# Half of the tokens first at the layer change, T's blocks by ScalarE's queue, and a new order of states, exponentials and the last gates

## The chip, the core and the metric

The kernel runs on one core of a Trainium2 chip. A core has five engines that each follow their own fixed list of instructions: TensorE (PE in the profile; PEld is its weight load), VectorE (DVE), ScalarE (ACT), GpSimd (POOL) and SyncE (SP), which only issues DMAs. ScalarE and GpSimd can issue DMAs as well. An instruction waits, by semaphores, until what it reads is there and what it overwrites has been read; what stands behind it on its engine waits with it. Matrix products go to PSUM (eight banks of 512 floats for each of 128 partitions), all else lies in SBUF or in HBM. The metric is the time of one execution on the device, in microseconds.

## The reference

512 tokens of 2048 floats pass two residual layers, x <- x + W_out(mixer(RMSNorm(x)) * silu(gate)), in float32. The first is differential attention with eight heads. The second is RWKV-7 time mixing with 32 heads of 64: one projection gives r, k, v, the gate g and two narrow streams of 96 columns (decay and learning rate), each mixed with the token before; then, for each head and token, a 64 x 64 state is updated.

```
p = h @ w_in;  p = p + (token_shift(p) - p) * mu
r, k, v, g, dw, da = split(p)
decay = exp(-exp(-softplus(-(w0 + tanh(dw) @ decay_up)) - 0.5))
a = sigmoid(a0 + da @ iclr_up)
kk = normalised(k * k_k);  k = k * (1 + (a - 1) * k_a)
S = S * decay + (S @ -kk) (kk * a)^T + v k^T;   y = S @ r      # token by token
y = group_norm(y) * gn_w + gn_b + sum(r * k * r_k) * v
x = x + (y * silu(g)) @ w_out
```

## The kernel before

**Products.** All large products take float32 data as a high and a low part in TensorE's reduced float32 format and make three products of them (`mm3`, L114): high x high, high x low, low x high. Weights come by SyncE's queue as 512 KB blocks (`wraw`), ScalarE casts the high part (`wh`, L102), VectorE subtracts it (`wl`, L103). The normalised activations stand as 16 blocks of 128 channels by 512 tokens (`hH`, `hL`), which both layers' projections read.

**Order.** A planner places each engine's instructions ahead of time by priorities: `high_priority(offset)` moves a piece forward by AHEAD (2000), SCAN (3000) or SOLVE (4000), and `issue_after` pins it behind an instruction. Work of the scan is strung in between the projections' products by a count: each `mm3` product is a tick, and a `Chain` makes its next step after a given number of ticks (L127 to L173).

**The start.** TensorE makes a few products of the identity (`warm`, L616) before the first block of x is there, two more after the first block's transposes.

**The layer change.** The last part of attention's W_out ends with `seven`, which forms half of the output columns by a scheme of seven block products; `store_x` stores each finished tile of the residual by ScalarE's queue (L725) and sums its squares on ScalarE (L727). VectorE makes the reciprocal root of the norm for tokens 0 to 255 and then for 256 to 511 (L774 to L777) and scales x by it (L770). `more_h` transposes a block of 128 channels, all four token tiles, on TensorE (L790); `make_h` writes hH on ScalarE (L811) and hL on VectorE (L812); `unit_chan` multiplies each block by the 192 columns of the two narrow streams (tile `lora`).

**A pair of heads.** Layer 1 goes over 16 pairs of heads. For pair j its k, r and v are projected, then `stage1` makes the decay's cumulative sums and exponentials; three pieces of it (`decays`, `queries`, `keys`) stand in a list `later`, and one piece is issued after each state of the scan that is running. `gram` multiplies keys and queries in chunks of 64 tokens (tile `gp`, L1021), copies the result to G on ScalarE (L1028), and sends six small pieces to HBM by GpSimd's queue (`ltd`, L1034 and L1040); GpSimd then masks G in four instructions (L1046, L1048). `t_solve` loads the pieces back in another layout by four DMAs of GpSimd (`LT`, L1071) and inverts triangular blocks of 32 in 31 steps of two VectorE instructions (`tmpl` L1082, `Tm` L1084); the result goes to HBM (`td`, L1086). In the next pair's turn `t_combine` loads it (`TT`, L1098, SyncE), transposes it on VectorE (L1106), multiplies on TensorE (`px`, L1112 and L1122), and copies back on ScalarE (L1115, L1118, L1125).

**The scan.** `scan_pair` walks over eight chunks. Each has a product (`sm`, L1193), its copy on ScalarE (`rhs`, L1196), a product with T (L1204), its copy (`VS`, L1206), a product (L1211) and the new state on VectorE, one instruction for each of two heads (L1215; L1218 in the first chunk), with a copy and a scaling on GpSimd (`SA` L1199, `Sg` L1202). `outputs` and `centre` follow, then `group_norm`, `finish_y` and the gate.

**The last projections.** After pair 15 the gates of pairs 13, 14 and 15 are projected and the rows of the gated output are split again into high and low parts (`split_row`, L421 and L422, into the buffers of hH and hL): rows 0 to 13 from HBM (`yr`), rows 14 and 15 from the gates directly. Then W_out is applied.

Of the kernel before, what the change touches and what calls it, by code (L numbers as in the profile page):

```python
# [23 lines left out]
P = 128  # L24
# [14 lines left out]
AHEAD, SCAN, SOLVE = 2000, 3000, 4000  # L39
# [552 lines left out]
def layer0(g, aps):  # L592
# [3 lines left out]
    with ExitStack() as cx:  # L596
# [46 lines left out]
        def more(n, m):  # L643
            for k in range(len(g.hH), min(n, KT)):
# [5 lines left out]
                if k == 0:  # L650
                    warm_up(2, last.ins)
# [27 lines left out]
    with ExitStack() as cx:  # L679
# [43 lines left out]
        def store_x(cb, t):  # L723
            xr = xs[cb][:, t, :]
            nc.scalar.dma_start(out=g.xd[t * P : (t + 1) * P, cb * 512 : cb * 512 + 512], in_=xr)  # L725
            junk = g.work.tile([P, 512], F32, name="junkx", tag="a", bufs=2)
            nc.scalar.activation(junk[:], xr, AF.Square, accum_out=g.ssx[:, t, cb : cb + 1])  # L727
# [77 lines left out]
def make_h(g, ps, col):  # L805

    nc = g.nc
    hh = g.hp.tile([P, T], F32R, name="hH", tag="hH")
    hl = g.hp.tile([P, T], F32R, name="hL", tag="hL")
    w = g.prm_a[:, col : col + 1]  # L810
    m = nc.scalar.activation(hh[:], ps[:], AF.Copy, scale=w)  # L811
    d = nc.vector.scalar_tensor_tensor(hl[:], ps[:], w, hh[:].bitcast(F32), ALU.mult, ALU.subtract)  # L812
    g.hH.append(hh)
    g.hL.append(hl)
    return m.ins, d.ins
# [128 lines left out]
def stage1(g, j, k, up):  # L944
# [24 lines left out]
    def decays():  # L969
# [3 lines left out]
        nc.vector.tensor_sub(l[:], l[:], m[:, :, None].to_broadcast([P, NC_, C]))  # L973
        nc.scalar.activation(p.E[:, :, 0], m[:], AF.Exp, scale=-1.0)
# [20 lines left out]
    g.later += [decays, queries, keys]  # L995
# [14 lines left out]
def gram(g, j, p, before):  # L1010
# [33 lines left out]
    for h in range(2):  # L1044
        r_ = slice(h * C, h * C + C)
# [16 lines left out]
def t_solve(g, j, p):  # L1062
# [7 lines left out]
    for i in range(NG):  # L1070
        nc.gpsimd.dma_start(out=LT[i * 32 : i * 32 + 32], in_=g.ltd[j % 2].rearrange("b h c s t -> (b h c) s t"))  # L1071
# [14 lines left out]
    nc.gpsimd.dma_start(out=g.td[j % 2].rearrange("q l t -> l q t"), in_=Tm[:])  # L1086

# [4 lines left out]
def t_combine(g, j, p):  # L1092
# [11 lines left out]
    for h in range(2):  # L1104
        r_ = slice(h * C, h * C + C)
        nc.vector.transpose(T1[r_], TT[r_, :, h, 0:HALF])  # L1106
# [47 lines left out]
def gate(g, j, gps):  # L1154
    nc, w = g.nc, g.work
    gt = shift_mix(g, gps, P, *mus(g, 3, j), "v", 1)
# [6 lines left out]
def gated(g, j, p, gt, last=False):  # L1163
    g.nc.vector.tensor_mul(gt[:], gt[:], p.y[:])
    if last:
        return split_row(g, gt[:])
# [15 lines left out]
def scan_pair(g, j, p, gap, gap_s, others):  # L1182
# [8 lines left out]
    for c in range(NC_):  # L1191
# [20 lines left out]
        for h, r_ in HEADS:  # L1212
            s_ = sm[r_, o + h * C : o + h * C + C]
            if c:
                g.state = nc.vector.scalar_tensor_tensor(VS[r_, c + 1, h, :], s_, p.gam[r_, c : c + 1], Sg[r_, :],  # L1215
                                                         ALU.mult, ALU.add)
            else:
                nc.vector.tensor_scalar(VS[r_, c + 1, h, :], s_, p.gam[r_, c : c + 1], None, ALU.mult)  # L1218
# [22 lines left out]
def centre(g, p):  # L1241
# [4 lines left out]
    for h in range(2):  # L1246
# [3 lines left out]
        nc.vector.tensor_sub(p.yc[:, h::2, :], yg, s1[:, :, h : h + 1].to_broadcast([P, NT, C]))  # L1250
# [25 lines left out]
def layer1(g, aps):  # L1276
    nc, tc = g.nc, g.tc
    with ExitStack() as cx:
# [23 lines left out]
        for j in range(D // P):  # L1302
# [13 lines left out]
            def behind(m, j=j, p=p):  # L1316
# [4 lines left out]
                t_solve(g, j, p)  # L1321
# [18 lines left out]
        gt = gate(g, j - 1, gps)  # L1340
        row = []

        def last_but_one(m):
            with tc.issue_after(m.ins):
                finish_y(g, j - 1, pairs[j - 1])
                row.append(gated(g, j - 1, pairs[j - 1], gt, True))

        gt = gate(g, j, proj(3, j, behind=(24, last_but_one)))
        rows = split_rows(g, g.yd2, ("r", "k", "th0", "th1", "l", "f", "xH", "xL"), 1, j - 1) + row

        def all_rows(n, _):
            if n >= KT and len(rows) < KT:
                group_norm(g, j, p)
                finish_y(g, j, p)
                rows.append(gated(g, j, p, gt, True))
# [56 lines left out]
def body(ctx, tc, nc, aps):  # L1412
    g = Ctx()
    g.nc, g.tc = nc, tc
    g.last, g.first = None, []
# [40 lines left out]
```

## Time and profile before

| what | before |
|---|---|
| median of three runs | 2207.12 us (2206.14 to 2209.69) |
| profiled execution | 2213.33 us, span 2211.6 us |
| mean granted TensorE clock | 0.990 |
| busy: TensorE, VectorE, ScalarE, GpSimd | 98%, 65%, 47%, 16% of the span |

The profile gives, for one execution, each engine's busy time, the waits by who ended them, and a timeline. A row of the timeline shows the start and length in us, engine, source line, operation, output and inputs, the shape, how many instructions are merged (x4), and in brackets the idle time of the engine before it and what ended that. Matmuls are pipelined, and their ends are modelled. The columns of the views that are quoted below are told where they stand.

### The profile page before, as it was taken

To read this page: it belongs to the slowest core of one execution; us is meant where nothing else is said; L and a number is where in the kernel's file an instruction comes from. 1 tells how busy PE (TensorE), PEld (TensorE's weight loads), DVE (VectorE), ACT (ScalarE), POOL (GpSimd) and SP (SyncE) were. 2 spreads that over 40 slices of the span, in tenths; PEclk is the share of its full clock that TensorE was granted. 3 is DMA by queue.
4 is the path that set the end of the run, shared out by engine and by line. 5 is a ranking of instruction groups with operands and counts; after the bars stand their busy time and mean duration, and the time that the engine had idled before them with its cause. 6 is when DMAs were issued, how large, how long until landed. Compare 5 with 4: busy or idle time off the path is not lost. (4 is left out here: it accounts for less than half of the span.)

```text
span 2211.6 us, 33922 instructions
## 1 busy us (share of the span) xinstructions
PE 2173.2 (98%) x12202; PEld 1762.5 (80%) x12202; DVE 1445.7 (65%) x3772; ACT 1040.9 (47%) x2110; POOL 359.8 (16%) x733
## 2 busy tenths in 40 slices
PE   9999999999999999989999999999999999999999
PEld 7888888888888878867777777778777777777887
DVE  5664646455564666465677788677777777777645
ACT  6443434344343454335455555555555556545322
POOL 0000000000000000110233233333332233331001
PEclk9999999999999999999999999999999999999999
DMA  6322232222222356643422333333333332345456
GB/s 192 97 85 97 77 102 89 87 95 86 96 86 95 129 183 213 162 106 90 106 67 78 79 92 86 82 91 94 98 91 82 89 88 75 107 131 182 174 166 120
DMA packets 281401, 240.21 MB, mean 109 GB/s; under 512 B 31792, under 2 KB 239744, under 8 KB 281232
## 3 DMA queue, kind: packets, MB, share of 16 engines
q1 hardware_dynamic: 256912, 190.13, 28.5%
q0 software_dynamic: 15456, 31.90, 6.7%
q10 hardware_dynamic: 8864, 16.01, 2.0%
q8 instruction: 96, 1.57, 0.3%
q14 instruction: 73, 0.60, 0.1%
HBM read 217.98 MB, written 19.99 MB: 108 GB/s over the span
## 5 line engine op out<-in xcount | busy, mean ns | idle before, releaser
L103 DVE TENSOR_TENSOR wl<-wraw,wh 128x1024 fp32r<-128x1024 f32 (+2 forms) x319 | 388.8, 1219 | 360.9 <-ACT wh L102 353.9
L102 ACT CAST wh<-wraw 128x1024 fp32r<-128x1024 f32 (+2 forms) x319 | 333.4, 1045 | 535.3 <-PE pp L114 374.5
L114 PE MATMUL pp<-wh,hH 128*128 128x512 f32 x1268 | 499.8, 394 | 4.0 <-ACT hH L421 2.4
L114 PE MATMUL pp<-wl,hH 128*128 128x512 f32 x1268 | 498.0, 393 | 0.0
L114 PE MATMUL pp<-wh,hL 128*128 128x512 f32 x1268 | 497.7, 393 | 0.0
L114 PE MATMUL pp<-hL,wh 128*128 128x512 f32 x1024 | 417.6, 408 | 0.0
L114 PE MATMUL pp<-hH,wl 128*128 128x512 f32 x1024 | 417.1, 407 | 0.0
L114 PE MATMUL pp<-hH,wh 128*128 128x512 f32 x1024 | 412.1, 402 | 0.0
L114 PEld LDWEIGHTS pp<-wh,hH 128*128 128x128 f32 x1268 | 238.6, 188 | 52.9 <-ACT hH L421 2.8
L114 PEld LDWEIGHTS pp<-wh,hL 128*128 128x128 f32 x1268 | 238.5, 188 | 47.9
L114 PEld LDWEIGHTS pp<-wl,hH 128*128 128x128 f32 x1268 | 238.8, 188 | 46.7
L114 PEld LDWEIGHTS pp<-hH,wh 128*128 128x128 f32 x1024 | 195.1, 191 | 37.0 <-issue 1.2
L114 PEld LDWEIGHTS pp<-hL,wh 128*128 128x128 f32 x1024 | 194.8, 190 | 35.2
L114 PEld LDWEIGHTS pp<-hH,wl 128*128 128x128 f32 x1024 | 195.0, 190 | 31.4
L1082 DVE SCALAR_TENSOR_TENSOR tmpl<-LT,Tm 128x60 f32<-128x60 f32 (+24 forms) x496 | 133.1, 268 | 10.6
L459 POOL DMA_DIRECT2D frow<-yd x12 | 8.9, 739 | 796.4 <-DVE rs_i L63 676.6
L1199 POOL COPY SA<-VS 64x64 f32<-64x64 f32 x224 | 61.2, 273 | 428.2 <-DVE VS L1215 382.9
L1084 DVE TENSOR_TENSOR Tm<-Tm,tmpl 128x60 f32<-128x60 f32 (+24 forms) x496 | 104.2, 210 | 11.2
L1215 DVE SCALAR_TENSOR_TENSOR VS<-sm,gam,Sg 64x64 f32<-64x64 f32 x192 | 54.2, 282 | 50.9 <-PE sm L1211 46.5
L1196 ACT COPY rhs<-sm 64x64 f32<-64x64 f32 x256 | 52.8, 206 | 63.6 <-PE sm L1193 61.1
L1206 ACT COPY VS<-sm 64x64 f32<-64x64 f32 x256 | 52.8, 206 | 62.0 <-PE sm L1204 58.3
L1202 POOL TENSOR_SCALAR Sg<-SA,gam 128x64 f32<-128x64 f32 x96 | 72.9, 759 | 9.3
(326 smaller groups left out, 3224.0 us busy)
## 6 DMA issues: line engine op xcount, KB each, us to landing
wraw<-in_rw_w_in_dram SPq DMA_DIRECT2D x128, 512.0 KB, 3.8
wraw<-in_da_w_in_dram SPq DMA_DIRECT2D x254, 256.0 KB, 2.9
wraw<-in_da_w_out_dram SPq DMA_DIRECT2D x26, 512.0 KB, 4.4
wraw<-in_rw_w_out_dram SPq DMA_DIRECT2D x26, 512.0 KB, 3.9
LT<-ltd POOLq DMA_DIRECT2D x64, 132.0 KB, 2.9
yr<-yd SPq DMA_DIRECT2D x28, 256.0 KB, 3.5
frow<-yd POOLq DMA_DIRECT2D x12, 512.0 KB, 6.9
xq<-in_x_dram SPq DMA_DIRECT2D x16, 256.0 KB, 5.7
```

The lines of the kernel that those rows point to most:

```text
L102: nc.scalar.copy(hi[:, ks], raw[:, ks])
L103: nc.vector.tensor_sub(lo[:, ks], raw[:, ks], hi[:, ks].bitcast(F32))
L114: m = nc.tensor.matmul(out, a, b, start=s, stop=e, skip_group_check=skip)
L459: nc.gpsimd.dma_start(out=r, in_=src[k0 * P : (k0 + KG) * P, :].rearrange("(k p) t -> p k t", p=P))
L1082: nc.vector.scalar_tensor_tensor(tt, LT[:, i : i + 1, i + 1 :].to_broadcast([P, s, n]), n2[:, i : i + 1], Tm[:, 0:s, i : i + 1].to_broadca ...
L1084: nc.vector.tensor_add(Tm[:, 0:s, i + 1 :], Tm[:, 0:s, i + 1 :], tt)
L1196: nc.scalar.copy(rhs[r_, :], sm[r_, h * C : h * C + C])
L1199: nc.gpsimd.tensor_copy(p.SA[r_, c - 1, :], VS[r_, c, h, :])
L1202: nc.gpsimd.tensor_scalar(Sg[:], p.SA[:, c - 1, :], p.gam[:, c : c + 1], None, ALU.mult)
L1206: nc.scalar.copy(VS[r_, c, h, :], sm[r_, P : P + C])
L1215: g.state = nc.vector.scalar_tensor_tensor(VS[r_, c + 1, h, :], s_, p.gam[r_, c : c + 1], Sg[r_, :], ALU.mult, ALU.add)
```

## The change

1. The warm-up behind the first transposes grows from two products to seven.
2. `store_x` sums the squares before it issues the store, and for the last 1024 columns with priority SCAN.
3. At the layer change the first eight blocks are made and multiplied for tokens 0 to 255, then for 256 to 511 (`half_h`, `products`); blocks 8 to 15 as before. A PSUM tile then holds two blocks of two token tiles.
4. The exponentials leave `decays` for a piece of their own (`exps`), so that `later` has four pieces.
5. The six stores of `gram` go by ScalarE's queue; the masks become `mask_gram`, called for one head before `t_solve` and for the other behind its loads.
6. T's transposes in `t_combine` are pinned behind the last `centre` of the scan before.
7. The new state is placed with priority STATE (8000), ahead of the rows of T (SOLVE, 4000).
8. The last gate has a buffer of its own (tag E), and the rows of pairs 14 and 15 are split inside W_out's first unit, row 14 once four blocks are asked for, row 15 at the end.

```diff
-                    warm_up(2, last.ins)
+                    warm_up(7, last.ins)
...
         def store_x(cb, t):
             xr = xs[cb][:, t, :]
+            junk = g.work.tile([P, 512], F32, name="junkx", tag="a", bufs=2)
+            with tc.high_priority(offset=SCAN if cb > 1 else 0):
+                nc.scalar.activation(junk[:], xr, AF.Square, accum_out=g.ssx[:, t, cb : cb + 1])
             nc.scalar.dma_start(out=g.xd[t * P : (t + 1) * P, cb * 512 : cb * 512 + 512], in_=xr)
-            junk = g.work.tile([P, 512], F32, name="junkx", tag="a", bufs=2)
-            nc.scalar.activation(junk[:], xr, AF.Square, accum_out=g.ssx[:, t, cb : cb + 1])
...
+        def half_h(k, half, m):
+            ps = g.ps.tile([P, 512], F32, name="xT", tag="pa", bufs=2)
+            for i in range(2):
+                xq, c0 = xs[(k + i) // 4], (k + i) % 4 * P
+                for t in range(2):
+                    tt, at = 2 * half + t, (2 * i + t) * P
+                    if c0 == 0 and half:
+                        scale((k + i) // 4, tt)
+                    with tc.issue_after(m.ins) if m else ExitStack():
+                        nc.tensor.transpose(ps[:, at : at + P], xq[:, tt, c0 : c0 + P], g.ident[:])
+            for i in range(2):
+                with tc.high_priority(offset=AHEAD):
+                    make_h(g, ps[:, 256 * i : 256 * i + 256], KT + k + i, k + i, half)
...
-        unit_chan(g, [(aps["rw_w_in"][0], 4 * D, 2 * RK)], 2 * RK, RK, more_h, pts=pts)
+        lora = [(aps["rw_w_in"][0], 4 * D, 2 * RK)]
+        def products(k, wt, s, m):
+            for c in range(2):
+                wh, wl = [x[:, k % 4, c * RK : (c + 1) * RK] for x in wt]
+                m = mm3(nc, pts[c][:RK, s], wh, wl, g.hH[k][:, s], g.hL[k][:, s],
+                        k == 0 and s.start == 0, k == KT - 1, g, True)
+            return m
+        m, wts = None, []
+        turns = [(k, half) for half in range(2) for k in range(0, KT // 2, 2)]
+        for i, (k, half) in enumerate(turns):
+            if i == 0:
+                half_h(k, half, m)
+            if i + 1 < len(turns):
+                half_h(*turns[i + 1], m)
+            else:
+                more_h(KT // 2 + 1, m)
+            if half == 0 and k % 4 == 0:
+                wts.append(split_w(g, lora, 4, 2 * RK, k))
+            for kk in (k, k + 1):
+                m = products(kk, wts[kk // 4], slice(256 * half, 256 * half + 256), m)
+        for k in range(KT // 2, KT):
+            if k % 4 == 0:
+                wts.append(split_w(g, lora, 4, 2 * RK, k))
+            more_h(k + 2, m)
+            m = products(k, wts[k // 4], slice(0, T), m)
...
         nc.vector.tensor_sub(l[:], l[:], m[:, :, None].to_broadcast([P, NC_, C]))
+
+    def exps():
         nc.scalar.activation(p.E[:, :, 0], m[:], AF.Exp, scale=-1.0)
...
-    g.later += [decays, queries, keys]
+    g.later += [decays, exps, queries, keys]
...
-        nc.gpsimd.dma_start(
+        nc.scalar.dma_start(
             out=g.ltd[j % 2, half, :, :, HALF, :],
...
-            nc.gpsimd.dma_start(
+            nc.scalar.dma_start(
                 out=g.ltd[j % 2, half, h, :, 0:HALF].rearrange("c s t -> s c t"),
...
-        nc.vector.transpose(T1[r_], TT[r_, :, h, 0:HALF])
+        with g.tc.issue_after(g.centred) if g.centred else ExitStack():
+            nc.vector.transpose(T1[r_], TT[r_, :, h, 0:HALF])
...
+            with g.tc.high_priority(offset=STATE):
+                if c:
+                    g.state = nc.vector.scalar_tensor_tensor(VS[r_, c + 1, h, :], s_, p.gam[r_, c : c + 1], Sg[r_, :],
+                                                             ALU.mult, ALU.add)
...
-                t_solve(g, j, p)
+                mask_gram(g, p, 0)
+                loaded = t_solve(g, j, p)
+                with tc.issue_after(loaded):
+                    mask_gram(g, p, 1)
...
-                row.append(gated(g, j - 1, pairs[j - 1], gt, True))
+                gated(g, j - 1, pairs[j - 1], gts[0], True)
...
-        gt = gate(g, j, proj(3, j, behind=(24, last_but_one)))
-        rows = split_rows(g, g.yd2, ("r", "k", "th0", "th1", "l", "f", "xH", "xL"), 1, j - 1) + row
+        gts.append(gate(g, j, proj(3, j, behind=(24, last_but_one)), "E"))
+        rows = split_rows(g, g.yd2, ("r", "k", "th0", "th1", "l", "f", "xH", "xL"), 1, j - 1)
         def all_rows(n, _):
+            if n >= 4 and len(rows) == KT - 2:
+                rows.append(split_row(g, gts[0][:]))
```

More of the change, by code (lines that the diff above doesn't have):

```diff
@@ L36 @@
     pass
-AHEAD, SCAN, SOLVE = 2000, 3000, 4000
+AHEAD, SCAN, SOLVE, STATE = 2000, 3000, 4000, 8000
 def ahead(offset):
@@ L1339, in layer1 @@
         group_norm(g, j - 1, pairs[j - 1])
-        gt = gate(g, j - 1, gps)
-        row = []
+        gts = [gate(g, j - 1, gps)]
         def last_but_one(m):
@@ L1414, in body @@
     g.nc, g.tc = nc, tc
-    g.last, g.first = None, []
+    g.last, g.first, g.centred = None, [], None
     g.chains, g.later, g.state = [], [], None
```

42 lines of the change are left out of this document (22 added, 20 removed).

## The prediction

> **What bounds the kernel now.** I read the page's busy shares first, then TensorE's own waits, then stretches with the granted clock, and last the timeline at the places that these name.
>
> ```profile
> span 2211.6 us, 33922 instructions
> PE 2173.2 (98%) x12202; PEld 1762.5 (80%) x12202; DVE 1445.7 (65%) x3772; ACT 1040.9 (47%) x2110; POOL 359.8 (16%) x733
> ...
> 334.38 0.28 PE L114 MATMUL o<-VL,at 128*128 128x256 f32 x1
> 334.50 0.28 PE L114 MATMUL o<-V,al 128*128 128x256 f32 x1
> ...
> L114 PE MATMUL pp<-wh,hH 128*128 128x512 f32 x1268 | 499.8, 394 | 4.0 <-ACT hH L421 2.4
> ```
>
> TensorE is the bound: 98% busy, no other engine above 65%. Nothing that it computes is taken away, so the change can only win back time in which it stands or runs slowly. The two rows of 256 columns are neighbours 0.12 us apart, each shown as 0.28 long: ends are modelled some 0.16 late, and each wait below costs about 0.16 more than is shown. A product of 512 columns, 0.394 in the last row, is then worth 0.23.
>
> ```profile
> PE px L1112 <- DVE T L1106: 7.4, 10, 2.4
> PE xT L790 <- DVE xq L770: 5.0, 1, 5.0
> PE sm L1211 <- ACT VS L1206: 4.2, 16, 0.7
> PE sm L1193 <- DVE VS L1215: 3.6, 15, 0.5
> PE pp L114 <- ACT hH L421: 2.4, 1, 2.4
> ```
>
> These columns are total us, times, longest. They name four places: T's transposes in front of the products px; the layer change (xT); the two state waits of the scan (sm); the change to the last projection (hH L421).
>
> ```profile
> 978.00:989.00 11.00, 5.33 (x19) 2.89 (x18) 10.33 (x30) 3.33 (x7) 0.00 (x0) 0.69 0.29 92
> 1095.00:1112.00 17.00, 14.59 (x94) 11.13 (x93) 3.65 (x6) 5.29 (x12) 5.62 (x12) 0.60 0.38 94
> 1204.00:1211.00 7.00, 5.55 (x47) 4.03 (x46) 2.88 (x6) 1.74 (x4) 6.35 (x13) 0.76 0.46 108
> 1388.00:1399.00 11.00, 10.26 (x110) 8.49 (x110) 3.63 (x6) 7.02 (x13) 3.44 (x6) 0.69 0.26 60
> 1763.00:1775.00 12.00, 10.97 (x114) 9.02 (x113) 4.55 (x7) 7.49 (x15) 4.36 (x7) 0.72 0.28 64
> 2026.00:2034.00 8.00, 5.60 (x20) 4.30 (x19) 5.49 (x9) 7.60 (x16) 0.00 (x0) 0.79 0.37 115
> 1576.00:1638.00 62.00, 61.52 (x423) 49.31 (x422) 47.74 (x130) 34.71 (x78) 19.48 (x42) 1.00 0.34 90
> ```
>
> The columns are the stretch, its length, busy time of PE, PEld, DVE, ACT and POOL, the granted clock, DMA. Length times missing clock is 11 x 0.31 = 3.4, 17 x 0.40 = 6.8, 7 x 0.24 = 1.7, 3.4, 12 x 0.28 = 3.4, 8 x 0.21 = 1.7: 20.4 us in all, each stretch at one of the places just named. A usual pair of heads (last row) takes 62 us with TensorE busy for 61.52 at full clock. So at most 22.6 us of waits, 43 x 0.16 = 6.9 behind them and 20.4 of clock can be won: 50.
>
> **Half of the tokens first.**
>
> ```profile
> 978.57 0.44 PE L790 MATMUL xT<-ident,xq 128*128 128x128 f32 x2
> 984.66 1.30 PE L790 MATMUL xT<-ident,xq 128*128 128x128 f32 x4 [4.97 <-DVE xq L770]
> 986.32 1.17 PE L114 MATMUL lora<-hH,wh 128*96 128x512 f32 x2 [0.35 <-ACT hH L811]
> 975.24 1.81 DVE L770 TENSOR_SCALAR xq<-xq,rs 128x512 f32<-128x512 f32 x4
> 980.39 0.19 ACT L727 ACTIVATION_READ_ACCUMULATOR junkx<-xq 128x1 f32 x1
> 989.43 0.69 ACT L811 ACTIVATE hH<-xT,prmin_norm_w_dram 128x512 fp32r<-128x512 f32 x1 [2.60 <-PE xT L790]
> ```
>
> Tokens 0 to 255 are scaled by 977.05 (four tiles, enough for eight of the 16 blocks), the others wait for the second half's root and a scaling, which lets go of TensorE at 984.66. The old order needs all four token tiles for the first block, so the first lora product comes at 986.32. In the new order the transposes of the first half can follow 978.57; ScalarE is free when its squares end at 980.58, a half-wide hH is about 0.5 (half of 0.69, and the fixed part), so products start at some 981.1, 5.2 earlier. From there cover is enough: eight blocks of six half-wide products at 0.12 are 5.8 us, past 984.66. 48 products become 96 half as wide: 96 x 0.12 against 48 x 0.23 is +0.5 at most, and I take nothing. Eight blocks also cost one ScalarE and one VectorE instruction more each, under TensorE's products. The squares ahead of the two stores on ScalarE's queue gain nothing by themselves, as stores under a running instruction cost nothing (row of L725 below). The clock fell at the gap; 2.5 us of transposes and waiting stay, so I leave the clock as it is. Ends: +2 and -8.6 (5.0 + 0.16 + 3.4). I take **-5**.
>
> **T's blocks by ScalarE's queue, masks split around the loads.**
>
> ```profile
> 1586.04 0.70 POOL L1046 TENSOR_SCALAR_AFFINE_SELECT G<-G 64x512 f32<-64x512 f32 x1
> 1589.63 1.99 POOL L1071 DMA_DIRECT2D LT<-ltd  x4
> LT<-ltd POOLq DMA_DIRECT2D x64, 132.0 KB, 2.9
> 1597.59 0.18 DVE L1073 TENSOR_SCALAR LT<-LT 128x32 f32<-128x32 f32 x1
> 1638.30 0.44 DVE L1106 STREAM_TRANSPOSE T<-TT 64x256 f32<-64x256 f32 x1 [1.04 <-DMA TT<-td]
> ```
>
> GpSimd has issued its six stores when the first of four masks starts at 1586.04; the four loads follow the masks at 1589.63, land 2.9 us after their issue, by 1594.5, and VectorE starts the solve at 1597.59. With the stores on ScalarE and two masks behind the loads, the loads can start 1 to 3 us earlier; I take 2, for the rows and for T's transposes. The ten px waits, 9.0 us with their hidden part, are mostly shorter than 2 us each: -8. With them go the clock losses at 1204, 1388 and 1763: 1.7 + 3.4 + 3.4 = 8.5. The first pair's wait is 2.4, so I leave its 6.8. Sum **-16.5**. Ends: 0, if the rows start no earlier, and 9.0 + 15.3 = -24.3. The masks now later are read by the next pair's scan, a pair (62 us) away. GpSimd's four loads now wait for a landing, and the copies of the states (SA, Sg), which VectorE's next state waits for, stand behind them as they stood behind masks and loads before. T's transposes put behind the centring cost nothing: in the row above they already come last.
>
> ```profile
> 961.73 1.01 ACTq L725 DMA_DIRECT2D xd<-xq  x2
> 962.65 0.63 ACT L727 ACTIVATE junkx<-xq 128x512 f32<-128x512 f32 x1
> L1098 SPq DMA_DIRECT2D TT<-td x64: 319/444/487, 1095.2 to 2012.0; - x64
> ```
>
> ScalarE gets 16 x 6 = 96 issues. A store of this shape takes SyncE's queue 444 ns, 42.6 us in all. The two issues of the row of L725 ended at 962.74, and ScalarE's next instruction started at 962.65 with no idle time before it: they delayed nothing. Behind them stand the copies rhs and VS of the scan and the cast wh, which TensorE waits for. Ends: 0 and +42.6; nearest is that row of L725, since ScalarE is busy for 34.71 of 62 us: I take a tenth, **+4**. The Trainium skill, page "DMA: Bandwidth & Descriptors", section "Issuing engines are not separate DMA queues", speaks against this edit: transfers from all queues share 16 DMA engines, only the time of the issue is saved. No row here compares two queues on one transfer. By that rule alone the loads move by two of the four masks, (1589.63 - 1586.04) / 2 = 1.8 us; the waits over 1.8 us keep a rest and the term would be about -16 in place of -16.5.
>
> **States ahead of T's rows, exponentials a state later.**
>
> ```profile
> 1612.49 0.22 ACT L974 ACTIVATE E<-m 128x8 f32<-128x8 f32 x1 [0.67 <-DVE m L972]
> 1613.22 0.49 PE L1211 MATMUL sm<-VS,BKT 128*128 128x128 f32 x2 [0.22 <-ACT VS L1206]
> 1620.41 0.26 DVE L1082 SCALAR_TENSOR_TENSOR tmpl<-LT,Tm 128x54 f32<-128x54 f32 x1
> 1621.14 0.46 PE L1193 MATMUL sm<-VS,G 128*128 128x128 f32 x2 [0.18 <-DVE VS L1215]
> ```
>
> ScalarE stood 0.67 for VectorE's m with the copy VS behind it; exponentials issued a state later find m done. On VectorE a row of T (0.26) went between the two halves of a state; with the higher priority it does not. The two rows of waits hold 4.2 + 3.6 + 31 x 0.16 = 12.8. I take half, **-6**; ends -12.8 and +5 (the keys come a state, some 6 us, later: after 1621 instead of before it, with the Gram products a third of a pair away).
>
> **The last projections.**
>
> ```profile
> 2029.14 0.50 PE L114 MATMUL pp<-wh,hH 128*128 128x512 f32 x1 [2.40 <-ACT hH L421]
> 2026.30 0.62 ACT L421 CAST hH<-mixv 128x512 fp32r<-128x512 f32 x1
> 2028.48 1.65 ACT L421 CAST hH<-yr 128x512 fp32r<-128x512 f32 x3
> ```
>
> The first row block for W_out (hH<-yr) is split behind that of the last pair but one (hH<-mixv), which waits for its scan; the change moves the latter behind, and gives the last gate its own buffer. The gap of 2.4 + 0.16 and the 1.7 of clock go, less a rest of 0.8: **-3.5**. Ends -4.3 and +1, if the split of the moved block is late next.
>
> **The start.** Five more warm-up products at the start are ten instructions.
>
> ```profile
> 5.69 0.61 PE L616 MATMUL warm<-ident 128*128 128x128 f32 x4
> 7.70 0.50 PE L114 MATMUL pp<-wh,hH 128*128 128x512 f32 x1 [1.40 <-ACT hH L811]
> ```
>
> Four take 0.61, so ten add at most 1.5, which ends before the hH that TensorE waits for at 7.70 (6.3 + 1.4). Nothing; +1 at half clock.
>
> **Sum.** -5 - 16.5 + 4 - 6 - 3.5 = -27. The profiled execution took 2213.33 (span 2211.6 and 1.7 around it), so 2186.3; it lies 6.2 above the median of 2207.12, which gives **2180**.
>
> **The rivals.** *T no earlier.* VectorE is busy for 47.74 of 62 us while the rows run, so the rows can start earlier and end where they did. For it: 3 us already lie between landing and first row. Against: VectorE's order is fixed ahead and shifts with the loads. Then -16.5 falls away: -10.5, 2196.6.
>
> *The clock goes down anyway.* The small products px and the Gram products would set it off, not the waits: at 1388 TensorE is shown busy for 10.26 of 11 us. Against: all 15 pairs have these products, four lost the clock. Then the 6.8 of 1388 and 1763 stay: -20, 2187. The Trainium skill, page "TensorE: Matmul & The Clock Gate", section "What's actually happening", lets the clock halve only after an idle window of about 3.4 us, which speaks for this rival at 1388 and 1763, where no such idle time stands. At the layer change the same rule would keep the clock up, as the gap falls from 5 us to under 3, and that term would be about -6.
>
> *ScalarE's queue as the new wait (slower).* The six issues stand in one queue with rhs, VS and wh just when the scan of the last pair starts. Decides from 27 + 4 = 31 us over 16 pairs: 1.9 us of the 2.7 a pair must reach TensorE. At all of it the sum is -31 + 42.6 = +11.6, 2219. For it: TensorE waits for the copy VS already (the row at 1613.22 above). Against: the row of L725.
>
> **How the numbers follow.** Forecast 0.45 (own range 2168 to 2190), T no earlier 0.22, clock 0.13, ScalarE's queue 0.15, the change undone by a new order of VectorE (within 4 us of before) 0.05. A measurement tells 0.2% (4.4 us) from no change. Faster: 0.45 + 0.22 + 0.13 = 0.80; same 0.05; slower 0.15. The range reaches from 2165 (the own sum with the first pair's 6.8 and more of the scan) to 2206, which leaves out the slower rival and little below.
>
> **What would show it.** After: xT's wait under 1 us and lora products by 982; loads LT within 8 us of the last Gram product and px waits under 2 us in all; clock 1.00 in the stretches of 1388 and 1763; the waits of sm halved; no wait on hH L421; ScalarE's issues with no idle time of TensorE behind them. The prediction is wrong if rhs or VS show up as TensorE's longest waits.

## The result: slower by 1.4%

The changed kernel takes 2238.46 us (median of 5 runs, 2232.75 to 2244.52), the kernel before 2206.73 on the same chip. The ratio is 1.0138, 95% interval [1.0125, 1.015]. The prediction was 2180, with a range up to 2206: wrong in sign. The profiled execution of the changed kernel is the one of 2238.46. Its span, 2236.8 us, is 25.2 longer than that of before (2211.6), whose profiled execution lay 6.2 above its median: the two traces show 25 of the 32 us.

### The profile after

The busy times in the changed kernel's page:

```profile
PE 2195.4 (98%) x12260; PEld 1784.7 (80%) x12260; DVE 1448.0 (65%) x3780; ACT 1045.1 (47%) x2118; POOL 285.1 (13%) x637
```

TensorE is busy for 98% of the span, as before, and 22.2 us longer (before 2173.2). The Gram products of the changed kernel, with the columns busy us, mean ns of one, and idle us in front with what ended it:

```profile
L1067 PE MATMUL gp<-AR,BK 64*128 64x128 f32 x512 | 49.0, 334 | 0.6 <-DVE AR L1051 0.6
```

The same of the kernel before:

```profile
L1021 PE MATMUL gp<-AR,BK 64*128 64x128 f32 x512 | 34.3, 286 | 1.4 <-DVE AR L1005 1.1
```

These products are the same in number and shape, yet they take 14.7 us more, and the wait in front of px is 11.5 us longer (18.9 in the next view, 7.4 before). The lost time lies where T meets the Gram products. TensorE's waits for T and in the scan in the changed kernel (total us, times, longest):

```profile
PE px L1163 <- DVE T L1157: 18.9, 19, 2.9
PE sm L1244 <- DVE VS L1267: 2.4, 12, 0.3
PE sm L1255 <- ACT rhs L1247: 2.2, 12, 0.2
...
PE sm L1262 <- ACT VS L1257: 1.2, 4, 0.6
```

The waits at the layer change (xT, 5.0) and at the last projection (hH L421, 2.4) are gone, and the three waits of the scan fell from 8.4 (4.2, 3.6 and 0.6) to 5.8: these went the way that was forecast, the scan's by a third and not by half. The px wait went the other way.

The view of the tile gp, first of the kernel before, then of the changed one; the last two times are the starts of the first and the last Gram product:

```profile
L1021 PE MATMUL gp<-AR,BK x512: 272/272/422, 1043.5 to 1956.8; 64*128 64x128 f32 x171
```

```profile
L1067 PE MATMUL gp<-AR,BK x512: 271/272/578, 1040.0 to 1984.8; 64*128 64x128 f32 x171
```

The first Gram product comes 3.5 us earlier, the last 28.0 later, the end 25.2 later. So the loss is in the 16 pairs of heads. One steady pair in the timeline of the changed kernel (start, us, engine, line, tile, count, and in brackets the idle time in front and what ended it): TensorE, then VectorE, then ScalarE's queue, then the loads on GpSimd's queue with VectorE's first row.

```profile
1593.91 0.69 PE L1163 MATMUL px<-T,G 32*32 32x32 f32 x16
1594.52 0.71 PE L1067 MATMUL gp<-AR,BK 64*128 64x128 f32 x6
1595.74 0.69 PE L1163 MATMUL px<-T,G 32*32 32x32 f32 x16 [0.51 <-DVE T L1157]
1596.36 1.82 PE L1067 MATMUL gp<-AR,BK 64*128 64x128 f32 x26
...
1593.42 0.44 DVE L1157 STREAM_TRANSPOSE T<-TT 64x256 f32<-64x256 f32 x1 [0.92 <-DMA TT<-td]
1593.79 0.64 DVE L1051 TENSOR_TENSOR AR<-mixr,E 128x512 f32<-128x512 f32 x1
1594.46 0.75 DVE L1052 SCALAR_TENSOR_TENSOR mixr<-mixr,prm_hrk,f 128x512 f32<-128x512 f32 x1
1595.24 0.44 DVE L1157 STREAM_TRANSPOSE T<-TT 64x256 f32<-64x256 f32 x1
...
1601.89 0.63 ACTq L1080 DMA_DIRECT2D ltd<-ssl  x1
1605.56 0.31 ACTq L1086 DMA_DIRECT2D ltd<-G  x1
...
1608.78 0.56 POOL L1120 DMA_DIRECT2D LT<-ltd  x1 [2.15 <-DMA ltd<-G]
1618.23 0.18 DVE L1122 TENSOR_SCALAR LT<-LT 128x32 f32<-128x32 f32 x1
```

The same place in TensorE's timeline of the kernel before:

```profile
1577.35 1.09 PE L1112 MATMUL px<-T,G 32*32 32x32 f32 x32
1578.37 2.06 PE L1021 MATMUL gp<-AR,BK 64*128 64x128 f32 x32
```

And in VectorE's timeline of the kernel before:

```profile
1575.98 0.44 DVE L1106 STREAM_TRANSPOSE T<-TT 64x256 f32<-64x256 f32 x1 [0.52 <-DMA TT<-td]
1576.35 0.70 DVE L854 SCALAR_TENSOR_TENSOR mixr<-pp,prmin_rw_mu_dram,mixr 128x511 f32<-128x511 f32 x1
1577.08 0.44 DVE L1106 STREAM_TRANSPOSE T<-TT 64x256 f32<-64x256 f32 x1
1577.55 0.69 DVE L1005 TENSOR_TENSOR AR<-mixr,E 128x512 f32<-128x512 f32 x1
```

Two instructions of VectorE write mixr: the first makes r out of the projection (mixr<-pp) and stands ahead of AR, the second stands behind AR. In what follows mixr is the first unless it is called the second.

Two things are new. VectorE's order at the Gram products is now mixr (at 1591.75), T, AR, the second mixr, T; before, it was T, mixr, T, AR and then the second mixr. The second half of px waits for a transpose that stands behind two other instructions, and the Gram products are cut in two, 6 and 26. And the loads LT start 1608.78 - 1594.52 = 14.3 us after the first Gram product; before, it was 1589.63 - 1578.37 = 11.3, and 2 less was forecast. ScalarE issues the last of its six stores only at 1605.56, behind copies and casts, and VectorE's first row starts 23.7 us after the first Gram product instead of 19.2.

Stretches around Gram products of the changed kernel (length, busy PE, PEld, DVE, ACT, POOL, granted clock, DMA):

```profile
1330.00:1338.00 8.00, 6.39 (x97) 5.89 (x98) 2.21 (x4) 4.13 (x9) 0.04 (x1) 0.79 0.33 80
1461.00:1471.00 10.00, 9.49 (x90) 7.99 (x90) 0.61 (x3) 5.98 (x14) 1.78 (x2) 0.66 0.20 54
1525.00:1540.00 15.00, 13.51 (x117) 11.17 (x116) 3.14 (x5) 6.77 (x14) 2.24 (x7) 0.66 0.20 47
1200.00:1950.00 750.00, 732.69 (x4871) 589.45 (x4869) 554.26 (x1512) 406.96 (x909) 170.89 (x422) 0.97 0.33 86
```

The same stretch of the kernel before:

```profile
1200.00:1950.00 750.00, 738.54 (x4992) 591.93 (x4991) 571.27 (x1558) 414.79 (x933) 236.79 (x509) 0.99 0.33 90
```

The clock now falls in these places, to 0.97 from 1200 to 1950, against 0.99 before.

### The profile page after: what moved, and what is told of

Read it like the earlier page. It is cut to its first block, busy times and chain, and to the rows that moved or that the text cites. A ratio compares the mean times of both kernels' runs of the same rounds, so it can differ in the third digit from the quotient of the medians.

```text
span 2236.8 us, 34056 instructions
## 1 busy us (share of the span) xinstructions
PE 2195.4 (98%) x12260; PEld 1784.7 (80%) x12260; DVE 1448.0 (65%) x3780; ACT 1045.1 (47%) x2118; POOL 285.1 (13%) x637
## 5 line engine op out<-in xcount | busy, mean ns | idle before, releaser
L1267 DVE SCALAR_TENSOR_TENSOR VS<-sm,gam,Sg 64x64 f32<-64x64 f32 x192 | 54.1, 282 | 22.2 <-PE sm L1262 17.8
L1255 PEld LDWEIGHTS sm<-rhs,TT 128*128 128x128 f32 x256 | 44.6, 190 | 28.4 <-ACT rhs L1247 21.1
```

The lines of the kernel that those rows point to most:

```text
L1255: nc.tensor.matmul(sm[:, P : P + C], both(g.TT[j % 2][:, c]), rhs[:], start=True, stop=True)
```

## The experiments

Each ratio is to the kernel before, run beside it on the same chip.

**Which part costs?** Four kernels. The first undoes the queue part in the changed kernel, the second makes it alone in the kernel before, the third makes the three order parts alone, the fourth the ends alone (warm-up, layer change, last projections).

```diff
# stores_on_gpsimd (from the changed kernel)
-        nc.scalar.dma_start(out=g.ltd...
+        nc.gpsimd.dma_start(out=g.ltd...
+                mask_gram(g, p, 1)        # ahead of t_solve again
# stores_on_scalar_only (from the kernel before): the same lines the other way
# order_only (from the kernel before)
+    g.later += [decays, exps, queries, keys]
+            with g.tc.high_priority(offset=STATE):   # VS on VectorE
+        with g.tc.issue_after(g.centred) ...:        # T's transposes
# ends_only: the changed kernel without any of the lines above, all masks ahead of the loads
```

> The changed kernel with its queue part undone: T's six stores a pair of heads go out by GpSimd again, and all four masks stand ahead of the loads LT, as before; the rest of the change stays. Theory 'late stores': on ScalarE's queue the six stores of a pair stand between wh casts and the copies rhs and VS, so their issue ends 11 to 15 us after the first Gram product instead of 7.5, the loads LT start at 14 to 18 us instead of 11, T comes late by as much, and TensorE meets T in the middle of the Gram products. Then this kernel has loads at about 11 us, px waits under 8 us in all, 2.0 us for the 32 Gram products of a pair, and takes 2185 to 2200. Rival 'order on VectorE': T's second transpose now stands behind AR and r (1.8 us behind the first, 1.1 before), and the states at high priority push the rows back; then the loads return to 11 us but the px waits stay above 12 us, and the time is 2220 to 2235.

Measured: 2225.22, 1.0073 [1.0058, 1.0088]. The loads start at 11 us again and the px waits are 13.6 us: the rival's numbers.

> The kernel before with the queue part alone (six stores a pair by ScalarE's queue, two masks ahead of the loads LT and two behind them). 'Late stores': loads LT 13 us or more after the first Gram product, px waits above 15 us in all, 2225 to 2245. 'Order on VectorE': 2200 to 2212, with px waits as before (7.4 us).

Measured: 2211.91, 1.0017 [1.0002, 1.0031]. The time is the rival's, but the px waits are 11.1 us and not 7.4.

> The kernel before with the order parts alone: exponentials a state later, states at high priority, T's transposes behind the centring; stores and masks as before. 'Late stores': the scan's waits shrink from 8.4 us to about 5.8 as they did in the changed kernel, T no later: 2198 to 2206. 'Order on VectorE': px waits above 12 us and 2220 to 2235.

Measured: 2231.75, 1.0105 [1.0088, 1.0122]. The time is the rival's, but the px waits are 10.9 us and not above 12.

> The kernel before with the ends alone: warm-up products, half of the tokens first at the layer change, the last gate's own buffer and its row block split later. Both theories: the layer change gains 5 to 9 us and the last projections 3 to 4: 2194 to 2200. If it gains under 3 us, the gain at the layer change or at the end is given back in the first pairs of heads.

Measured: 2201.65, 0.9969 [0.9958, 0.998].

The order parts cost most; my theory of late stores, formed on the trace above, does not carry the loss. The queue part alone costs 0.2%. The ends gain 0.3%, less than expected. The rival's times came, and so did the longer rows that it named (34.7 us a pair in both kernels with the states' priority, 34.2 before), but not its order. VectorE's second transpose of T and AR in order_only:

```profile
1589.88 0.44 DVE L1109 STREAM_TRANSPOSE T<-TT 64x256 f32<-64x256 f32 x1
1590.36 0.69 DVE L1007 TENSOR_TENSOR AR<-mixr,E 128x512 f32<-128x512 f32 x1
```

The transpose stands ahead of AR, as before, in 11 of the pairs, in stores_on_gpsimd too, and the Gram products are cut in one pair only. What these two kernels lose is not lost by a new order at the Gram products.

**Which of the order parts, and is the late half of the stores' work better?**

```diff
# states_only
+            with g.tc.high_priority(offset=STATE):
# exps_only
+    g.later += [decays, exps, queries, keys]
# transposes_only
+        with g.tc.issue_after(g.centred) if g.centred else ExitStack():
# ends_and_late_stores (from ends_only)
+        (nc.scalar if j > 3 else nc.gpsimd).dma_start(out=g.ltd...   # and mask_gram(g, p, 1) behind the loads there
```

> The kernel before with one of the three order parts alone: the state updates of the scan at high priority on VectorE. In the run with all three, the 95 VectorE instructions from the first row of T to the last took 34.72 us a pair in place of 34.23, the two halves of a state going as a pair of 0.60 us in place of two single ones between rows. Theory 'states': these 0.5 us and the waits behind them are the cost, T's last row ends 1 us later, and this kernel alone takes 2218 to 2232. Theory 'keys': the cost comes from the exponentials; then this kernel takes 2200 to 2212.

Measured: 2216.26, 1.0041 [1.0028, 1.0055], between the two ranges.

> The kernel before with the exponentials a state later alone. In the run with all three order parts the queries and keys came some 6 us later, after 33.8 of the rows' 34.7 us began to run out, and the last keys (BK) stood between the last rows. 'Keys': T's last row ends 1 us later for that, 2215 to 2230. 'States': the rows keep their 34.2 us and their end at 51.4 us after the first Gram product, 2200 to 2212.

Measured: 2238.02, 1.0133 [1.0117, 1.0149].

> The kernel before with T's transposes behind the centring alone. They stood last already, so both theories expect 2203 to 2211 and px waits as before; 2215 or more would make this part the cause, by T's second transpose behind AR and r.

Measured: 2209.93, 1.0006 [0.9996, 1.0015].

> The ends alone (2201.65) plus the queue part from the fifth pair of heads on (pairs 0 to 3 keep GpSimd's stores and all masks ahead of the loads). With the queue part alone the stretch from Gram 2 to Gram 4 took 125.8 us instead of 120.2, and that from Gram 5 to Gram 15 615.4 instead of 627.7 (621.5 with the ends alone). If both hold here, the loss of the first pairs is avoided and about 6 us are gained over the ends alone: 2192 to 2198. If the gain of the late pairs was the clock's alone (no half clock in them), 2199 to 2206.

Measured: 2201.70, 0.9968 [0.9959, 0.9977]: no gain over the ends alone.

The exponentials a state later cost as much as the whole change. "Keys" named the part, but neither its time nor its mechanism: T's last row ended earlier, not later (in most pairs 52.6 us after the first Gram product, 53.1 to 53.4 before). TensorE's waits in exps_only:

```profile
PE px L1114 <- DVE T L1108: 11.7, 10, 2.6
PE gp L1023 <- DVE AR L1007: 9.9, 12, 1.1
```

VectorE's timeline of exps_only in front of a Gram:

```profile
1594.54 0.44 DVE L1108 STREAM_TRANSPOSE T<-TT 64x256 f32<-64x256 f32 x1 [3.88 <-DMA TT<-td]
1594.91 1.18 DVE L103 TENSOR_TENSOR wl<-wraw,wh 128x1024 fp32r<-128x1024 f32 x1
1596.12 0.44 DVE L1108 STREAM_TRANSPOSE T<-TT 64x256 f32<-64x256 f32 x1
1596.59 0.75 DVE L854 SCALAR_TENSOR_TENSOR mixr<-pp,prmin_rw_mu_dram,mixr 128x511 f32<-128x511 f32 x1
1597.37 0.69 DVE L1007 TENSOR_TENSOR AR<-mixr,E 128x512 f32<-128x512 f32 x1
```

VectorE stands 3.88 us at T's transpose, which waits for its load, and wl, mixr and AR, which were ahead of it or between, now stand behind. So TensorE stops 12 times at the Gram products for AR. The planner put VectorE's instructions in another order, one that fits a T that is there sooner than on the chip; that it reckoned with such a T is my inference.

The states' priority leaves VectorE's order at the Gram products as it was. Its price is in VectorE's rows: from the first start to the last end they take 34.75 us in a pair of states_only (1633.71 - 1598.96), before 34.23 (1631.82 - 1597.59), and T is later by as much.

**Is T's chain as long as TensorE's pair?** Four kernels: the changed one with the exponentials undone; the ends with the masks split and GpSimd's stores; and the kernel before with T earlier and with T later.

```diff
# after_without_exps (from the changed kernel)
-    g.later += [decays, exps, queries, keys]
+    g.later += [decays, queries, keys]
# ends_and_masks (from ends_only)
+                loaded = t_solve(g, j, p)
+                with tc.issue_after(loaded):
+                    mask_gram(g, p, 1)
# fewer_rows (from the kernel before)
-    for i in range(HALF - 1):
+    for i in range(21):
# longer_T (from the kernel before), behind Tm's last multiplication
+    for _ in range(3):
+        nc.vector.tensor_scalar(Tm[:], Tm[:], 1.0, None, ALU.mult)
```

> The changed kernel with its exponentials back in one piece with the decays; all else of the change stays. Theory 'exponentials': alone they cost 30 us, the other parts alone +4 (stores), +8 (states), +2 (transposes) and -6.5 (ends), which add up to 2216; this kernel takes 2208 to 2222. Rival 'T's chain': from one Gram to the next T's chain takes as long as TensorE's work, so any delay of T (here the later loads and the longer rows) makes T's second transpose stand behind AR, stops TensorE inside the Gram products (2.6 to 4.5 us for 32 in place of 2.0) and lowers the clock there, with the exponentials or without; then 2224 to 2240.

Measured: 2217.48, 1.0031 [1.0017, 1.0045]. The exponentials cost about 1.1% in the changed kernel too. Its Gram products are still cut, with 18.3 us of px waits, and VectorE's order is that of the changed kernel. So there the exponentials do not cost by the order. Its granted clock is 0.991 to 0.994 in six runs, the changed kernel's 0.982 to 0.987 in five; why the exponentials lower it there stays open.

> The ends alone (2201.65) and the masks split around the loads LT, with GpSimd's stores as before: the loads can start two masks (1.8 us) earlier, about 9.2 us after the first Gram product in place of 10.9, without ScalarE. 'T's chain': T's rows end 1 to 2 us earlier, the px waits (7.2 us) fall below 4, 2192 to 2199. If GpSimd's queue gives the time back (loads waiting for the landing of the stores with the states' copies behind them), 2200 to 2206.

Measured: 2220.87, 1.0047 [1.0025, 1.007], 0.8% over the ends alone. Neither theory had this. T's rows end earlier (52.2 us after the first Gram product in the seventh pair, 53.1 in the ends alone) until the waits for AR begin, and VectorE's order is that of exps_only (T, wl, T, mixr, AR). Two rows of its timeline:

```profile
1572.60 0.44 DVE L1154 STREAM_TRANSPOSE T<-TT 64x256 f32<-64x256 f32 x1 [4.41 <-DMA TT<-td]
1572.96 1.18 DVE L103 TENSOR_TENSOR wl<-wraw,wh 128x1024 fp32r<-128x1024 f32 x1
```

TensorE's wait for AR in ends_and_masks, and the stretch from 1200 to 1950:

```profile
PE gp L1065 <- DVE AR L1049: 10.1, 12, 1.1
...
1200.00:1950.00 750.00, 732.16 (x4852) 589.29 (x4849) 550.39 (x1533) 410.21 (x920) 229.92 (x489) 0.97 0.33 87
```

The clock is 0.97 there and 1.00 in the ends alone: 750 x 0.03 = some 22 us, no less than the whole 0.8%.

> The kernel before with rows 21 to 30 of T's solve left out (20 VectorE instructions a pair, about 4.5 us), so that T is there earlier; its output is not that of the reference. It bounds what an earlier T can give. 'T's chain': no px waits from the fourth pair on, no half clock at 1391 and 1767, 2184 to 2196. If T's lateness does not set the time, 2202 to 2208.

Measured: 2197.39, 0.9946 [0.9929, 0.9963], between the two ranges. The kernel leaves out rows 21 to 30 of T's solve, so its output is not that of the reference; the rows take 22.5 us a pair, 11.7 less and not 4.5. No px wait is left among TensorE's waits. The scan's whole stretch in fewer_rows, with the clock in the third column from the end:

```profile
1000.00:2010.00 1010.00, 994.16 (x6690) 787.39 (x6688) 702.82 (x1736) 557.55 (x1227) 321.68 (x659) 1.00 0.36 95
```

About 0.5% was to be had from an earlier T.

> The kernel before with three multiplications of Tm by 1 put behind its last one, which lengthens T's chain by about 1 us a pair and leaves TensorE's work as it is. 'T's chain': T's second transpose gets behind AR, the Gram products are split, 2218 to 2240, as in the changed kernel without any of its edits. If T has 1 us to spare in most pairs, 2206 to 2212.

Measured: 2219.35, 1.0046 [1.0031, 1.0061]. A microsecond more in T's chain puts T's second transpose behind AR and cuts the Gram products (2 and 30), much as in the changed kernel: the place tips with one microsecond.

**Is it the order?** The transposes bound behind r's VectorE instruction, which gives wl, mixr, T, T, AR, and nothing else touched:

```diff
# exps_T_behind_r (from exps_only); the same lines in ends_masks_T_behind_r (from ends_and_masks),
# ends_T_behind_r (from ends_only) and all_but_queue_states (from the changed kernel with
# GpSimd's stores, without STATE; here in place of issue_after(g.centred))
+        with g.tc.issue_after(g.mixr):               # g.mixr: r's last instruction in shift_mix
             nc.vector.transpose(T1[r_], TT[r_, :, h, 0:HALF])
```

> The exponentials alone again (2238), with T's two transposes bound behind r's VectorE instruction (mixr), so that VectorE's order in front of a Gram is wl, mixr, T, T, AR in place of T, wl, T, mixr, AR. Theory 'order in front of the Gram': the 30 us came from T's first transpose standing ahead of wl and mixr and waiting 3.9 us for its load, so that AR came 0.8 us late in 12 pairs and the clock fell; this kernel has no AR waits worth speaking of and takes 2198 to 2212. Rival 'keys': the queries and keys, some 6 us later, cost it wherever T's transposes stand; then 2225 to 2240.

Measured: 2219.87, 1.0057 [1.0035, 1.0078], between the two ranges.

> The ends and the masks split (2220.9) with the same binding of T's transposes. 'Order in front of the Gram': the AR waits (10.1 us) go and the loads that start 1 us earlier are kept, 2190 to 2201. Rival 'GpSimd's queue': loads that stand behind the states' copies give back what the masks gave, 2205 to 2222.

Measured: 2188.98, 0.9911 [0.9889, 0.9934]. This beats both kernels.

> The changed kernel with GpSimd's stores and without the states' priority, T's transposes bound behind r in place of behind the centring: ends, split masks and exponentials a state later. 'Order in front of the Gram': each part can pay once the order is held, and this is at least as fast as the ends alone: 2186 to 2200. Rival 'keys': 2215 or more.

Measured: 2197.10, 0.9954 [0.9939, 0.9969].

> The ends alone (2201.65) with the same binding, as the measure for the two kernels above. Its order had one transpose between wl and mixr; both theories: 2198 to 2205.

Measured: 2199.66, 0.9959 [0.9945, 0.9972].

All_but_queue_states is the whole change without the queue and the states' priority, with that order held: 0.5% faster than before where the change as it stands is 1.4% slower. That takes three things away at once. The changed kernel with the binding and nothing else was not run, and the binding would not hold the order there by itself: in scalar_stores_T_behind_r, below, AR again stands ahead of T's second transpose. Where the order wasn't broken, as in the ends alone, the binding does little (0.9969 to 0.9959).

For the masks it is the order, wholly: 1.0047 becomes 0.9911, and against the ends with the same binding the split masks gain 0.5%. VectorE's timeline of ends_masks_T_behind_r in the same place:

```profile
1625.69 1.23 DVE L103 TENSOR_TENSOR wl<-wraw,wh 128x1024 fp32r<-128x1024 f32 x1 [2.19 <-ACT wh L102]
1626.83 0.74 DVE L898 SCALAR_TENSOR_TENSOR mixr<-pp,prmin_rw_mu_dram,mixr 128x511 f32<-128x511 f32 x1
1627.49 0.43 DVE L1155 STREAM_TRANSPOSE T<-TT 64x256 f32<-64x256 f32 x1
1628.57 0.44 DVE L1155 STREAM_TRANSPOSE T<-TT 64x256 f32<-64x256 f32 x1 [0.64 <-DMA TT<-td]
1629.04 0.69 DVE L1049 TENSOR_TENSOR AR<-mixr,E 128x512 f32<-128x512 f32 x1
```

And its stretch from 1200 to 1950, with a clock of 1.00:

```profile
1200.00:1950.00 750.00, 742.93 (x5136) 596.86 (x5135) 566.26 (x1578) 421.97 (x952) 240.90 (x521) 1.00 0.35 93
```

For the exponentials it is a little more than half: 1.33% becomes 0.57%. In the traces much of the rest lies in the first pairs. The stretch from the third Gram to the fifth, first in the kernel before:

```profile
1144.00:1265.00 121.00, 116.99 (x830) 91.65 (x828) 93.38 (x268) 66.34 (x153) 39.17 (x90) 0.99 0.32 81
```

And in exps_T_behind_r:

```profile
1147.00:1276.00 129.00, 122.55 (x829) 94.40 (x829) 92.66 (x262) 67.14 (x154) 38.90 (x90) 0.95 0.31 80
```

Eight microseconds more, 5 of them by the clock (129 x 0.05 against 121 x 0.01). The exponentials cost about as much with split masks and the order held: all_but_queue_states differs in them alone from ends_masks_T_behind_r and takes 8.1 us more. The same stretch, first in ends_masks_T_behind_r, then in all_but_queue_states:

```profile
1141.00:1259.00 118.00, 114.92 (x824) 90.34 (x824) 90.25 (x264) 66.17 (x153) 39.22 (x90) 1.00 0.32 83
```

```profile
1140.00:1268.00 128.00, 122.81 (x825) 96.26 (x825) 90.69 (x261) 66.31 (x153) 38.21 (x90) 0.92 0.32 82
```

Both traces with the exponentials are of executions above their kernel's median (2228.40 and 2203.60), so the clock's share may be theirs alone. What makes T late in those early pairs was not settled.

**What T and the queue are worth by themselves.** The kernel before with the split masks and the binding; the second of the two has T's stores on ScalarE's queue and is else the same.

```diff
# masks_T_behind_r: the lines of ends_and_masks and of the binding, in the kernel before
# scalar_stores_T_behind_r: these and
-        nc.gpsimd.dma_start(out=g.ltd...
+        nc.scalar.dma_start(out=g.ltd...
```

> The kernel before with the split masks and T's transposes bound behind r, without the ends and with GpSimd's stores. With the ends it took 2188.98, the ends with the binding alone 2199.66. If the split masks pay through an earlier T whatever else is there, the same 10.7 us come off the kernel before: 2194 to 2200. If they need the ends, 2202 to 2212.

Measured: 2200.43, 0.9961 [0.9947, 0.9976], 0.4 us above the first range.

> As the kernel beside it, but with T's stores on ScalarE's queue, as in the change: the only difference is the queue. 'Late stores': the loads LT start 2 us later (12.3 in place of 10.1 us after the first Gram product), T's second transpose stands behind AR again, and this takes 8 to 20 us more than the kernel beside it. If the queue is free, the two differ by under 4 us.

Measured: 2210.95, 1.0005 [0.9992, 1.0019].

The queue costs 0.44%, about 10 us. One pair of masks_T_behind_r in the timeline: its first Gram products, and the loads on GpSimd.

```profile
1572.30 1.94 PE L1021 MATMUL gp<-AR,BK 64*128 64x128 f32 x30
...
1582.42 1.99 POOL L1074 DMA_DIRECT2D LT<-ltd  x4 [0.48 <-issue]
```

The same of scalar_stores_T_behind_r:

```profile
1581.96 2.06 PE L1021 MATMUL gp<-AR,BK 64*128 64x128 f32 x32
...
1594.77 0.56 POOL L1074 DMA_DIRECT2D LT<-ltd  x1 [2.31 <-DMA ltd<-G]
```

With GpSimd's stores the loads start 10.1 us after the first Gram product (1582.42 - 1572.30), with ScalarE's 12.8 (1594.77 - 1581.96), behind the landing of a store. In most pairs it is 10.1 and 12.2 to 12.4, and T's last row ends at 52.2 and 53.8.

## Why the prediction was wrong

**The step that failed: "Nothing that it computes is taken away, so the change can only win back time".** It priced each edit by the stall it names and left the rest where it was. Two terms of the sum came out with the other sign for it: T's blocks (-16.5) and the states and exponentials (-6). The exponentials, the split masks and the queue each also moved T's transposes against wl, mixr and AR on VectorE, and the states' priority made T later by half a microsecond. The rival "the change undone by a new order of VectorE" named the place, but with "within 4 us of before" and a chance of 0.05; one such order cost 30 us (ends_and_masks, 1.0047, against 0.9911 with the binding). The prediction's own sign of being wrong, rhs or VS as TensorE's longest waits, did not come.

**The layer change, -5: right.** The wait is gone. The first lora product starts at 982.28 (986.32 before, "some 981.1" forecast), though TensorE comes to this place 1.3 us later (its last product z starts at 979.37, 978.08 before), and the first Gram comes 3.5 us earlier. The clock, 0.69 there before, is 1.00 from 974 to 985.5; the prediction had left it as it was.

**T's blocks, -16.5: wrong sign in this change, too large at its best.** "the loads can start 1 to 3 us earlier; I take 2" was wrong in the place that mattered: they start 3.0 us later. The wait for a landing had been counted, the way of six stores through ScalarE's order of copies and casts had not. With GpSimd's stores and split masks the loads do start about 1 us earlier, the rows end earlier too, against the rival "T no earlier", and with the order held that is worth 0.4 to 0.5%, some 9 to 11 us; fewer_rows bounds an earlier T at about 0.5%. "T's transposes put behind the centring cost nothing" held alone (1.0006).

**ScalarE's 96 issues, +4: under-sized, 10.** The measured price lies inside the bounds (0 to 42.6), but not by the way that the prediction looked at: TensorE's waits for the copies rhs and VS come to 3.4 us, 4.8 before (rhs alone 2.2, 0.6 before, but 4.8 with GpSimd's stores). What was queued behind was T itself. The rival "ScalarE's queue as the new wait", with 2219, had the sign right and the place wrong. The Trainium skill, page "DMA: Bandwidth & Descriptors", section "Issuing engines are not separate DMA queues", says that another engine's queue saves only issue time. The runs agree as far as they go: on ScalarE's queue the loads behind the stores start no earlier but 2.7 us later (12.8 against 10.1).

**States ahead, exponentials later, -6: the waits fell, the time rose.** The scan's waits fell from 8.4 to 5.8 us. But the exponentials alone cost 30 us, a little more than half by the order and the rest in a way that is not settled; the bound "+5 (the keys come a state, some 6 us, later: ...)" was for the keys and not for what was planned around them. The states' priority costs 0.4%; what the trace shows for it is 0.5 us of VectorE more a pair in T's chain, which has none to spare.

**The last projections, -3.5: the wait went, the gain did not.** Its 2.4 us are gone; but T came late in the last pair too, and between the last Gram product and the end only 2.8 us were made up. Layer change and last projections together gave 6.6 us in ends_only, against 8.5 forecast.

**The clock.** "The clock goes down anyway" falls: in fewer_rows all small products and Gram products are there, no px wait is, and the clock is 1.00 from 1000 to 2010. It goes with the waits, as the sum had it; they grew. It does not go by their sum alone: longer_T has 12.1 us of waits for T and AR, 8.5 in the kernel before, and its runs have the same mean clock of 0.994 as those beside them.

**The sum of single parts.** With VectorE's order at the Gram products held or unchanged, the exponentials cost 11.8 us (exps_T_behind_r), the states' priority 8.3, the transposes' binding behind the centring 2.0 (not clear of noise), and the ends give 6.6: 15.5 in all. Stores_on_gpsimd, which has these four and the order of before, lost 17.0. The queue part is then the last 14.7 of the change's 31.7 us, though alone it cost 3.7. Alone, it puts T's second transpose behind AR, and two pairs have their Gram products cut; in the changed kernel the transpose stands behind the second mixr too, 12 pairs are cut and the clock is lower. That these make 14.7 out of 3.7 was not tested by itself, and the parts do not simply add: the exponentials taken out of the changed kernel bring 1.1%, twice their 0.57% with the order held.

## What to carry to other kernels

When a transfer's chain from one use to the next is as long as the bound engine's work, as T's is here, move nothing near it without looking at the order that each engine then has in front of the meeting point: an instruction that waits for the transfer must stand behind what the bound engine needs before it, and ahead of what that engine needs later. Here one line that binds T's transposes behind r turned the split masks from +0.47% (with the ends) to -0.89%. And ask of a store moved to another queue not what its issue costs there, but what stands ahead of it.

## What the runs showed of the hardware

The low clock comes in pieces of one length. In the stretches after, length times missing clock, doubled because the clock goes to half (it is 0.50 from 1464 to 1468, inside the second): 8 x 0.21 x 2 = 3.4, 10 x 0.34 x 2 = 6.8, 15 x 0.34 x 2 = 10.2: one, two and three times 3.4 us. The Trainium skill, page "TensorE: Matmul & The Clock Gate", section "What's actually happening", gives a free-running window of 3413 ns, with which these pieces agree. The same section lets the clock fall after an idle window of that length; the changed kernel's trace shows no such idle time at these places: its longest px wait is 2.9 us.

The time of an issue on ScalarE's queue does not go by the bytes: 0.31 us for the 32 KB store ltd<-G, 0.63 for the 2 KB store ltd<-ssl (rows at 1605.56 and 1601.89). The nearest row that the prediction had, 0.444 on SyncE's queue, lay between.

Cutting 32 Gram products into 6 and 26, with 16 px between, costs more than the wait shown: from the first px to the products behind the last, 1598.11 - 1593.91 = 4.2 us against 1580.36 - 1577.35 = 3.0 before (1580.36 is the start of the next products px), with 0.51 shown as waiting.
